# Hyena's filter blocks in single-bank PSUM tiles, its VectorE chain cut finer, and other planner settings, in a one-core hybrid diffusion step

## The chip, the core and the metric

The kernel runs on one core of one Trainium2 chip, as one program. The time is device microseconds (us) of one execution. TensorE (PE in the profile) does the matmuls, VectorE (DVE), ScalarE (ACT) and GpSimd (POOL) the elementwise work, and SyncE (SP) issues the DMAs. Three runs took 1736.06, 1741.65 and 1744.64 us; the median is 1741.65 us.

## The reference

One step of a small backbone with two layers, on 512 latent tokens and 128 context tokens of width 1024 (640 rows, five token tiles of 128). Layer 0 mixes by attention (4 query heads, 2 key/value heads, each 128 wide, with q/k normalisation and rotary) beside a Hyena operator (512 channels); layer 1 is an mLSTM matrix memory with 8 heads, scanned in both directions. Each layer ends with a gated feed-forward block of width 2816. Cut to what the change touches:

```python
proj = x @ w_in                                # q, k, v of the attention and u of Hyena
q = rms_norm(proj[..., :A_Q].reshape(B, L, A_HEADS, A_HEAD_DIM), q_norm)   # k likewise
h = jnp.sin(sin_freq[1] * (h @ w2 + b2))       # Hyena's filters: a small MLP over positions
filt = (h @ w3 + b3).reshape(L, 2, HY_CH) * window[:, None, :]
y = long_conv(v, h_f) + flip(long_conv(flip(v), h_b)) + skip * v    # v = v * x1
out = concatenate([attn, y * x0]) @ w_out
# layer 1, per head and direction, in chunks of 64:
num = w_inter * (C @ q) + (w_intra * (q @ k.T)) @ v
h = num / maximum(abs(den), exp(-mt))
out = (rms_norm(h_f + rev(h_b)) * sigmoid(o)) @ w_out
# both layers: shift, scale and gate rows from silu(c) @ w_mod + b_mod, six sections per layer
```

## The kernel before

All matrix products run in three passes: each fp32 operand is split into a high part (made by ACT, `wh`, `a0h`) and a low part (made by DVE, `wl`, `a0l`), and PE multiplies high by high, high by low and low by high. So PE needs for each 128x1024 block of weights a DMA (`wr`), an ACT cast (`wh`) and a DVE subtraction (`wl`) first.

The stages follow each other on PE: the modulation rows of layer 0 (`mod`), Hyena's twelve projections of 128 channels each (`u4`, `u8`, `u5`, ... for the gate and value, then, after the q/k/v projection `qkv`, `u0` to `u3`), the attention (`s` scores, `pt` transposes of the probabilities, `po` outputs), the output projection, the feed-forward block of layer 0 (`u`, `g`, `dn` there), the mLSTM's projections head by head (`mq`, `mk`, `mo`) with the scans between them, its output projection `o10` onwards, and the feed-forward block of layer 1.

The order of instructions is made when the program is built, by a planner inside the kernel (class `Order`, from L60). It keeps a modelled clock for each engine. The main stream is a list of tasks that issue matmuls (`fm_first`, `fm_task`, `tm_tasks`). Beside it run "sides", generators that issue other work and `yield` between steps: `filter_block` (L1180, Hyena's filters), `forward` (L1112) and the rest of Hyena's long convolution, `qkv_evac` (L1399, the q/k normalisation), the chain of modulation sections (`spawn_mods`, L916), `direction` (L1788, one mLSTM scan) and others. A side's next step is issued once the modelled clocks of DVE and ACT are no further ahead of PE's than the side's lead (`when`, L164). `pump` (L191) starts a further main task early if DVE and ACT are less than a bound ahead; that bound is `TIGHT` while an urgent side is alive. `yield "mm"` and `yield "aux"` wait for a free PSUM tile: there are three two-bank tiles (`mm`) and two single-bank tiles (`aux`), and `od.gave` returns one.

Five places matter for the change. `filter_block` makes `hyf0` to `hyf4`: two matmuls of the filter MLP's last layer, 512 columns each, and two DVE multiplications by the window into `hs` and `hd`. `fm_first` (L523) runs the first three projections (u4, u8, u5) row block by row block, k by k, because its inputs come one k at a time; only the last `TAILK` k are done tile by tile. `forward`, called by `long_conv` with `inverse`, computes the transform of the values; `qkv_evac` evacuates the q/k/v product of a token tile, sums squares on ACT, makes the reciprocal root on DVE (`qn3v` to `qn3y`, eleven small operations) and scales. `direction` makes for head h and direction d the decay weights (`mb`, `w`), the carried state (`dl`, `cb`), the state's part of the output (`it`), the part within the chunk (`in`), the denominator, the sum `hs` and the final state (`pc`); when both directions of a head are done, `head_mix` (L1866) normalises `hs` (`hss`, `hn`), transposes it (`hT`) and multiplies it by the output gate (`mos`).

Of the kernel before, what the change touches and what calls it, by code (L numbers as in the profile page):

```python
# [15 lines left out]
ALU = mybir.AluOpType  # L16
# [43 lines left out]
class Order:  # L60
# [7 lines left out]
    LEAD = 3000.0  # L68
    SPARE = 5000.0
    GUARD = 0.0  # L70
    TIGHT = 2000.0
    FIRST = 2500.0

    def __init__(self):
# [116 lines left out]
    def pump(self):  # L191
        while True:
# [7 lines left out]
            else:  # L200
                spare = self.TIGHT if self.urgent else self.SPARE
                if self.urgent:
# [123 lines left out]
def hybrid_step(ctx: ExitStack, tc: tile.TileContext, A: dict, O: dict):  # L326
    od = Order()
    nc = Bunch(tc.nc, od)
# [16 lines left out]
    def page(name, dt=F32):  # L345
        return pp.tile([P, 648], dt, tag="pg", name=name)
# [7 lines left out]
    def mm(name):  # L354
        t = mmp.tile([P, 1024], F32, tag="mm", name=name)
        od.got("mm", t)
        return t

    def aux(name):
        t = auxp.tile([P, 512], F32, tag="aux", name=name)  # L360
        od.got("aux", t)
        return t

    def MM(out, lhsT, rhs, start=True, stop=True):
        r = nc.tensor.matmul(out, lhsT, rhs, start=start, stop=stop)  # L365
        n = 1
        for d in rhs.shape[1:]:
            n *= d
        k = lhsT.shape[0] / P
        if rhs.dtype == FR:  # L370
            od.issue("PE", max(57.0, 0.4453 * n + 4.0), [out], [lhsT, rhs], 162.0, n / 2.4 * k)
        else:
            od.issue("PE", 2 * max(112.0, n / 1.2 + 4.0), [out], [lhsT, rhs], 165.0, n / 0.6 * k)
# [23 lines left out]
    def rsqrt(ss, n, scale, name, eps=EPS, v=None):  # L397
        y, q, a = (small(name + c, n) for c in "yqa")
        if v is None:
            v = small(name + "v", n)  # L400
            nc.vector.tensor_scalar(v, ss, scale, eps, op0=ALU.mult, op1=ALU.add)
        nc.vector.tensor_scalar(y.bitcast(I32), v.bitcast(I32), -0.5, RSQ, op0=ALU.mult, op1=ALU.add)
        nc.vector.scalar_tensor_tensor(q, v, -0.5, y, op0=ALU.mult, op1=ALU.mult)
        for n in range(3):
            nc.vector.tensor_tensor(a, q, y, op=ALU.mult)
            if n < 2:
                nc.vector.scalar_tensor_tensor(q, a, 1.5, q, op0=ALU.add, op1=ALU.mult)
            nc.vector.scalar_tensor_tensor(y, a, 1.5, y, op0=ALU.add, op1=ALU.mult)
        return y
# [17 lines left out]
                yield  # L427

    EVF = 1
    TAILK = 3  # L430

    def fm_task(src, act, name, evac, needs=()):
        def run(w):
# [89 lines left out]
    def fm_first(specs, act):  # L523
# [9 lines left out]
        def all_(_):  # L533
            ps = []
            for n in range(3):
                od.take("mm")
                ps.append(mm(specs[n][1]))
            seq = [(k, n) for k in range(KT - TAILK) for n in range(3)]
            seq += [(k, n) for n in range(3) for k in range(KT - TAILK, KT)]
            for k, n in seq:  # L540
# [368 lines left out]
    HYE = nc.vector  # L909
    ROPE = nc.gpsimd  # L910
    SLACK1 = 1500.0
    SLACK2 = 2000.0
    SLACK3 = 500.0
    SLACK4 = 500.0

# [110 lines left out]
    def boundary(pss, tiles, l, s, xs, nxt, name, key, pages=None):  # L1026

        n = len(tiles)
        ss = small(name + "ss", n)
        t = {}  # L1030
        yield [("mod", l, s)] + [("mod", 1, 4)] * (l == 0 and s == 5)
        junk = page(name + "j").bitcast(BF)[:, 0:D]
        if WARM and tiles[0] == 0 and nxt is not None:
            nc.scalar.activation(ones1, ones[:, 0:1], AF.Gelu if s == 2 else AF.Exp)
        for j, i in enumerate(tiles):
            if nxt is not None and i >= ROWS:
                t[i] = mw.tile([P, D], F32, tag="mw", name=f"{name}t{i}")
            else:
                t[i] = row(f"{name}t{i}")
            nc.scalar.activation(junk, pss[i], AF.Square, accum_out=ss[:, j : j + 1])  # L1040
            nc.vector.tensor_tensor(t[i], pss[i], mods[l, s, 0 if i < 4 else 1], op=ALU.mult)
            od.gave("mm", pss[i])
            yield 0
        od.side_after(ss)
        yield
        r = rsqrt(ss, n, 1.0 / D, name)
        for j, i in enumerate(tiles):
            nc.vector.scalar_tensor_tensor(xs[i], t[i], r[:, j : j + 1], xs[i], op0=ALU.mult, op1=ALU.add)
            yield 0
            if nxt is None:  # L1050
                nc.sync.dma_start(O["y"][i * P : (i + 1) * P, :], xs[i])
        if nxt is None:
            return
        yield from pre_norm(xs, tiles, l + (s == 5), 3 if s == 2 else 0, nxt, name + "n", key, t, pages)
# [51 lines left out]
    def block(b):  # L1106

        return slice(LS, T) if b == 4 else slice(b, LS, 4)

    hy = {}  # L1110

    def forward(src, cols, out, name):  # L1112
# [24 lines left out]
        for n, (o, x, y, op) in enumerate(((out[0][:, a], c[:, a], c[:, b], ALU.add), (out[0][:, b], c[:, a], c[:, b], ALU.subtract),  # L1137
# [5 lines left out]
            nc.vector.tensor_tensor(o, x, y, op=op)  # L1143
            if FINE and n % FINE == FINE - 1:
                yield 0
        yield

    FINE = 0

    def filters():  # L1150
        z, w = hy["z"], hy["w"]
# [28 lines left out]
    def filter_block(b):  # L1180
        yield ["sin"]
        c = slice(0, HC)
        yield "mm"
        ps = mm(f"hyf{b}")
        for n in range(2):
            MM(ps[:, n * 512 : n * 512 + 512], hy["h"][:, block(b)], hy["w3s"][:, n * 512 : n * 512 + 512])
        load_win(b + 2)
        s_, d_ = page(f"hs{b}"), page(f"hd{b}")
        nc.vector.tensor_tensor(s_[:, c], ps[:, 0:512], hy["win"][b][:, c], op=ALU.mult)
        nc.vector.tensor_tensor(d_[:, c], ps[:, 512:1024], hy["win"][b][:, c], op=ALU.mult)  # L1190
        od.gave("mm", ps)
        hs.append(s_)
        hd.append(d_)

# [2 lines left out]
    def load_win(b):  # L1197
        if b < 5:
            hy["win"][b] = page(f"win{b}")
            nc.sync.dma_start(hy["win"][b][:, 0:HC], A["hy_win"][b])  # L1200
# [111 lines left out]
    def long_conv(hf):  # L1312
# [17 lines left out]
        HYE.tensor_tensor(vp[:, h1], vp[:, h1], gr, op=ALU.mult)  # L1330
        if FINE:
            yield 0
# [8 lines left out]
        for n in range(2):  # L1341
# [4 lines left out]
            HYE.tensor_tensor(S, S, gc, op=ALU.mult)  # L1346
            if FINE:
                yield 0
            nc.vector.tensor_tensor(x[0], x[0], x[1], op=ALU.subtract)
            nc.vector.tensor_tensor(C, C, S, op=ALU.add)  # L1350
            if FINE:
                yield 0
# [41 lines left out]

    QROWS = 2
    QACT = 1
    QSCALE = 1

    def qkv_evac(ps, i):  # L1399
        yield [("qk", j) for j in range(i - QROWS)]  # L1400
# [18 lines left out]
        r = rsqrt(ss, 6, 1.0 / DH, f"qn{i}")  # L1419
        if QSCALE:  # L1420
            for a in range(6):
# [116 lines left out]
    def out_proj(mix, wname, order, l, nxt, xs, halves, name):  # L1538
# [9 lines left out]
        for t in tm_tasks(  # L1548
                lambda k, i, g: [x[:, i * P : (i + 1) * P] for x in cur[k]],
                lambda k: A[wname][order[k] * P : (order[k] + 1) * P, :], KT, halves, name,  # L1550
                lambda ps, t: od.spawn(boundary(ps, t, l, 2, xs, nxt, f"{name}p{t[0]}", "af", name),
                                       lead=BLEAD, urgent=True),
                prep=prep, needs=lambda k, g: [key(q) for q in range(KT)], stay=STAY[l], whole=True,
# [312 lines left out]
    def head_mix(h):  # L1866
# [30 lines left out]
        for d in range(2):  # L1897
            od.spawn(direction(h, d, q, v1, kw[d], ssb, cb[d], hs, co), lead=DLEAD)
        yield [("hs", h)]
# [56 lines left out]
    J1 = 1  # L1956
    QLEAD = 6000.0
    ALEAD = 6000.0
    BLEAD = 4000.0
    FLEAD = 1000.0  # L1960
    MLEAD = 2500.0
    TLEAD = 1500.0
    DLEAD = 1750.0
    OLEAD = 5000.0
    ms = [x for i in range(4) for x in (4 + i, 8 + i)]
    k0, k1 = act_keys("am", 0, HALVES[0]), act_keys("am", 0, HALVES[1])
# [35 lines left out]
    act2 = Lazy("a2")  # L2002
    tasks.append(spawn_mods(SLACK2, (1, 0), (1, 1), (0, 5), (1, 3), (1, 4), keys=[("hid", 0, J0)]))
    tasks += ffn(0, act1, act2, xs)
# [299 lines left out]
```

## Time and profile before

| what | value |
|---|---|
| median of three runs | 1741.65 us |
| the profiled execution | 1739.15 us |
| its span, first to last instruction | 1737.3 us |
| mean granted TensorE clock | 0.987 of full speed |
| PE busy | 1683.4 us, 97% |
| DVE busy | 1243.6 us, 72% |
| ACT busy | 746.3 us, 43% |
| POOL busy | 353.8 us, 20% |

Busy time is the time in which an engine executes; register, branch and semaphore instructions don't count. In the slices of the page each digit is the busy share of one fortieth of the span in tenths. A row of a timeline gives start, duration, engine, line, operation, output and inputs; in square brackets stands how long the engine was idle before it and which engine's result ended that. Nearly all lines are those of helpers (L365 the matmul, L284 everything else), so rows are told apart by the names of their tiles. Granted clock 1.00 is 2.4 GHz and 0.50 is 1.2 GHz.

### The profile page before, as it was taken

To read this page: it belongs to the slowest core of one execution; us is meant where nothing else is said; L and a number is where in the kernel's file an instruction comes from. 1 tells how busy PE (TensorE), PEld (TensorE's weight loads), DVE (VectorE), ACT (ScalarE), POOL (GpSimd) and SP (SyncE) were. 2 spreads that over 40 slices of the span, in tenths; PEclk is the share of its full clock that TensorE was granted. 3 is DMA by queue.
4 is the path that set the end of the run, shared out by engine and by line. 5 is a ranking of instruction groups with operands and counts; after the bars stand their busy time and mean duration, and the time that the engine had idled before them with its cause. 6 is when DMAs were issued, how large, how long until landed. Compare 5 with 4: busy or idle time off the path is not lost. (4 is left out here: it accounts for less than half of the span.)

```text
span 1737.3 us, 25489 instructions
## 1 busy us (share of the span) xinstructions
PE 1683.4 (97%) x10074; PEld 1523.0 (88%) x10074; DVE 1243.6 (72%) x2057; ACT 746.3 (43%) x1233; POOL 353.8 (20%) x187
## 2 busy tenths in 40 slices
PE   7899899999999999999999999997999999999997
PEld 2778787789999999888899999996899999998886
DVE  4788797878878888797766888886578744445365
ACT  3422545545434344455565344334354423333343
POOL 0000121001546454340013111120015411111000
PEclk9999999999999999999999999998999999999999
DMA  9245132412434434454523212122124322223343
GB/s 359 91 152 170 37 101 101 169 38 99 158 121 143 144 119 154 153 198 129 188 89 137 70 47 83 57 69 100 49 77 147 125 77 74 73 74 109 132 159 122
DMA packets 64352, 203.85 MB, mean 117 GB/s; under 512 B 7335, under 2 KB 12455, under 8 KB 64234
## 3 DMA queue, kind: packets, MB, share of 16 engines
q1 hardware_dynamic: 64234, 202.23, 33.9%
q8 instruction: 79, 1.29, 0.3%
q14 instruction: 39, 0.32, 0.1%
HBM read 196.17 MB, written 3.94 MB: 115 GB/s over the span
## 5 line engine op out<-in xcount | busy, mean ns | idle before, releaser
L284 DVE TENSOR_TENSOR wl<-wr,wh 128x1024 fp32r<-128x1024 f32 (+1 forms) x260 | 317.9, 1228 | 107.8 <-ACT wh L284 107.6
L284 ACT CAST wh<-wr 128x1024 fp32r<-128x1024 f32 (+1 forms) x260 | 263.5, 1018 | 146.7 <-PE dn L365 104.1
L284 POOL TENSOR_TENSOR hid<-zg,zu 128x640 f32<-128x640 f32 x44 | 105.5, 2398 | 318.5 <-DVE zu L284 305.9
L284 DVE SCALAR_TENSOR_TENSOR acc<-mw,sc,acc 128x1024 f32<-128x1024 f32 x91 | 168.3, 1868 | 2.7 <-DMA mw<-in_w_mod 2.4
L284 POOL TENSOR_TENSOR acc<-acc,modp 128x1024 f32<-128x1024 f32 x49 | 146.2, 2984 | 115.4 <-ACT modp L284 91.2
L284 DVE SCALAR_TENSOR_TENSOR zg<-g,vec,zg 128x127 f32<-128x127 f32 (+3 forms) x168 | 87.4, 541 | 89.4 <-ACT zg L284 86.4
L365 PE MATMUL dn<-wh,hh 128*128 128x512 f32 x440 | 139.1, 396 | 1.8 <-DVE zu L284 1.6
L365 PE MATMUL dn<-wl,hh 128*128 128x512 f32 x440 | 138.2, 394 | 0.0
L365 PE MATMUL dn<-wh,hl 128*128 128x512 f32 x440 | 138.1, 394 | 0.0
L284 DVE SCALAR_TENSOR_TENSOR zu<-u,vec,zu 128x511 f32<-128x511 f32 (+2 forms) x164 | 86.7, 549 | 62.8 <-ACT zu L284 59.9
L284 ACT ACTIVATE zu<-u,vec 128x640 f32<-128x640 f32 (+1 forms) x42 | 36.8, 876 | 173.8 <-PE u L365 173.8
L365 PE MATMUL u<-a3h,wh 128*128 128x384 f32 (+1 forms) x336 | 104.7, 312 | 0.8 <-DVE a3h L284 0.8
L365 PE MATMUL g<-a3h,wh 128*128 128x384 f32 (+1 forms) x336 | 104.8, 312 | 0.0
L365 PE MATMUL g<-a1h,wh 128*128 128x384 f32 (+1 forms) x336 | 104.8, 312 | 0.0
L365 PE MATMUL u<-a3l,wh 128*128 128x384 f32 (+1 forms) x336 | 104.1, 310 | 0.5 <-POOL a3l L284 0.5
L365 PE MATMUL u<-a3h,wl 128*128 128x384 f32 (+1 forms) x336 | 104.3, 310 | 0.2 <-DVE wl L284 0.2
L365 PE MATMUL u<-a1h,wl 128*128 128x384 f32 (+1 forms) x336 | 104.2, 310 | 0.2 <-DVE wl L284 0.2
L365 PE MATMUL u<-a1h,wh 128*128 128x384 f32 (+1 forms) x336 | 104.2, 310 | 0.0
L365 PE MATMUL g<-a3h,wl 128*128 128x384 f32 (+1 forms) x336 | 104.1, 310 | 0.0
L365 PE MATMUL g<-a3l,wh 128*128 128x384 f32 (+1 forms) x336 | 104.1, 310 | 0.0
L365 PE MATMUL g<-a1h,wl 128*128 128x384 f32 (+1 forms) x336 | 104.0, 310 | 0.0
L365 PE MATMUL u<-a1l,wh 128*128 128x384 f32 (+1 forms) x336 | 104.0, 310 | 0.0
(742 smaller groups left out, 4452.2 us busy)
## 6 DMA issues: line engine op xcount, KB each, us to landing
wr<-in_w_up SPq DMA_DIRECT2D x92, 512.0 KB, 3.3
wr<-in_w_down SPq DMA_DIRECT2D x82, 512.0 KB, 3.3
mw<-in_w_mod SPq DMA_DIRECT2D x80, 512.0 KB, 4.4
wr<-in_w_ml SPq DMA_DIRECT2D x34, 512.0 KB, 3.6
wr<-in_w_out SPq DMA_DIRECT2D x18, 512.0 KB, 4.2
wr<-in_w_in SPq DMA_DIRECT2D x13, 512.0 KB
wr<-in_w_u SPq DMA_DIRECT2D x12, 512.0 KB, 5.2
we<-in_w_mod SPq DMA_DIRECT2D x8, 512.0 KB, 7.3
```

What stands on the lines that cost most here:

```text
L284: r = f(*args, **kw)
L365: r = nc.tensor.matmul(out, lhsT, rhs, start=start, stop=stop)
```

## The change

Seven numbers change, and the body of `filter_block`.

`filter_block` no longer takes one two-bank tile for both halves. It takes a single-bank `aux` tile, issues one 512-column matmul, the multiplication by the window, gives the tile back and yields, and then does the same for the other half. `FINE` 0 to 2 makes `forward` yield after every second of its eight DVE operations, and the rest of the long convolution yield between its parts, so that the planner may put other work in between. `QSCALE` 1 to 0 scales q and k of a token tile by one DVE tensor_tensor of 128x768 instead of six ACT operations of 128x128. `TAILK` 3 to 2: in `fm_first` only the last two k are done tile by tile. `TIGHT` 2000 to 6000, `SLACK2` 2000 to 4000, `BLEAD` 4000 to 6000 and `DLEAD` 1750 to 4000 (all in ns of the modelled clock) let main tasks, the modulation sections (1,0), (1,1), (0,5), (1,3), (1,4), the output projection's boundary and the mLSTM's scans be issued while DVE and ACT are modelled further ahead of PE.

```diff
-    TIGHT = 2000.0
+    TIGHT = 6000.0
...
-    TAILK = 3
+    TAILK = 2
...
-    SLACK2 = 2000.0
+    SLACK2 = 4000.0
...
-    FINE = 0
+    FINE = 2
...
     def filter_block(b):
         yield ["sin"]
         c = slice(0, HC)
-        yield "mm"
-        ps = mm(f"hyf{b}")
-        for n in range(2):
-            MM(ps[:, n * 512 : n * 512 + 512], hy["h"][:, block(b)], hy["w3s"][:, n * 512 : n * 512 + 512])
         load_win(b + 2)
         s_, d_ = page(f"hs{b}"), page(f"hd{b}")
-        nc.vector.tensor_tensor(s_[:, c], ps[:, 0:512], hy["win"][b][:, c], op=ALU.mult)
-        nc.vector.tensor_tensor(d_[:, c], ps[:, 512:1024], hy["win"][b][:, c], op=ALU.mult)
-        od.gave("mm", ps)
+        for n, t in enumerate((s_, d_)):
+            yield "aux"
+            ps = aux(f"hyf{b}{n}")
+            MM(ps, hy["h"][:, block(b)], hy["w3s"][:, n * 512 : n * 512 + 512])
+            nc.vector.tensor_tensor(t[:, c], ps, hy["win"][b][:, c], op=ALU.mult)
+            od.gave("aux", ps)
+            yield 0
...
-    QSCALE = 1
+    QSCALE = 0
...
-    BLEAD = 4000.0
+    BLEAD = 6000.0
...
-    DLEAD = 1750.0
+    DLEAD = 4000.0
```

Since the planner decides the order, the diff alone does not show where instructions go. Three places follow.

**The head, PE.** The first rows of PE before, from the modulation row products (`mod`; `we6`, `we7` are blocks of their weights) to the sums of squares of the inputs (`xss`):

```order
L365 MATMUL mod001_230<-we5_131,sc_93 2x512 x2
L365 MATMUL hyf0_248<-hyw3s_245,hyh1_193 128x512 x2
L365 MATMUL mod001_230<-we6_140,sc_93 2x512 x2
L365 MATMUL mod001_230<-we7_142,sc_93 2x512 x2
L365 MATMUL modt00_275<-vec_84,modr00_121 128x2 x8
```

The same place after the change, and further down, among the first projections (`u8` is tile u8_393; a0h, a0l and wh344, wl345 its operands):

```order
L365 MATMUL mod001_230<-we5_131,sc_93 2x512 x2
L365 MATMUL mod001_230<-we6_140,sc_93 2x512 x2
L365 MATMUL mod001_230<-we7_142,sc_93 2x512 x2
L365 MATMUL modt00_263<-vec_84,modr00_121 128x2 x8
L365 MATMUL xss_284<-ones_88,xq_233 128x1 x5
...
L365 MATMUL u8_393<-a0l0_373,wh1_344 128x384
L365 MATMUL hyf00_412<-hyw3s_245,hyh1_193 128x512
L365 MATMUL hyf01_415<-hyw3s_245,hyh1_193 128x512
```

`hyf0` has left its place between two row products and stands behind the first nine matmuls of the projections; `hyf1` and `hyf2` (not shown) go from behind u4's last matmul into the middle of these projections.

**Hyena's second half, DVE.** Before, from the third part of u0's convolution (`zh0`) to the low part of the weights of u3 (`wl24`); `vx01` to `vm11` are the second half's products with the filter spectrum (`g1c`, `g1s`) and their sums:

```order
L284 SCALAR_TENSOR_TENSOR zh0_1913<-u0_1820,vec_84,zh0_1913 128x127 x2
L284 TENSOR_TENSOR qsq3_1779<-qsq3_1779,qkg_1121 128x768
L284 TENSOR_TENSOR vx01_1873<-vf12_1597,g1c_953 128x512
L284 TENSOR_TENSOR vx11_1874<-vf13_1598,g1s_972 128x512
L284 TENSOR_TENSOR vf12_1597<-vf12_1597,g1s_972 128x512
L284 TENSOR_TENSOR vf13_1598<-vf13_1598,g1c_953 128x512
...
L284 TENSOR_TENSOR vm11_1972<-vf12_1597 128x256
L284 SCALAR_TENSOR_TENSOR zh1_2001<-u1_1919,vec_84,zh1_2001 128x511 x2
L284 SCALAR_TENSOR_TENSOR zh1_2001<-u1_1919,vec_84,zh1_2001 128x127 x2
L284 TENSOR_TENSOR wl24_2015<-wr24_1757,wh24_2014 128x1024
```

The same stretch after the change:

```order
L284 TENSOR_TENSOR qsq4_1802<-qsq4_1802,qn4y_1869 128x768
L284 SCALAR_TENSOR_TENSOR zh0_1903<-u0_1806,vec_84,zh0_1903 128x511 x2
...
L284 TENSOR_TENSOR wl23_1917<-wr23_1720,wh23_1916 128x1024
L284 TENSOR_TENSOR vp01_1947<-vx01_1769 128x256
...
L284 TENSOR_TENSOR qsq3_1791<-qsq3_1791,qkg_1126 128x768
L284 TENSOR_TENSOR qsq4_1802<-qsq4_1802,qkg_1126 128x768
L284 SCALAR_TENSOR_TENSOR zh1_1991<-u1_1909,vec_84,zh1_1991 128x511 x2
L284 SCALAR_TENSOR_TENSOR zh1_1991<-u1_1909,vec_84,zh1_1991 128x127 x2
L284 TENSOR_TENSOR wl24_2005<-wr24_1747,wh24_2004 128x1024
L284 TENSOR_TENSOR vx01_1769<-vf12_1634,g1c_955 128x512
L284 TENSOR_TENSOR vx11_1770<-vf13_1635,g1s_974 128x512
L284 TENSOR_TENSOR vf12_1634<-vf12_1634,g1s_974 128x512
```

`wl24` now stands ahead of the second half's four products with g1, their two sums and the four `vp` and `vm` operations instead of behind these ten; the normalisation of the last token tile (`qsq4`) has come forward, and `wl23`, which stood well ahead of `zh0` before, stands behind it.

**The end of the mLSTM, PE.** Before, from the last matmul of the last gate projection (`mo7`) to the first of the output projection (`o10_0`); `modp` are products for modulation section (1,2):

```order
L365 MATMUL mo7_11153<-a2l7_7690,wh154_10884 128x256
L365 MATMUL in71_11233<-v17_9003,w71_10986 128x129 x4
L365 MATMUL pc71_11254<-kw71_10839,v17_9003 128x128
L365 MATMUL pc71_11254<-v17_9003,kw71_10839 128x1
L365 MATMUL modp1200_11282<-moda120_11262,onesr_91 128x512
L365 MATMUL modp1200_11282<-modb120_11263,onesr_91 128x512
L376 MATMUL hT7_11286<-ident_86,hs7_10917 128x128 x5
L365 MATMUL modp1201_11303<-moda120_11262,onesr_91 128x512
L365 MATMUL modp1201_11303<-modb120_11263,onesr_91 128x512
L365 MATMUL o10_0_11311<-wh155_11016,o1h0_11020 128x512 x2
```

After the change, first where the last head's `in71` has gone (the middle of `mo5`, two gate projections earlier), then the end itself:

```order
L365 MATMUL mo5_10963<-a2l3_7502,wh152_10738 128x256
L365 MATMUL in71_11038<-v17_8988,w71_10933 128x129 x4
L365 MATMUL mo5_10963<-a2h4_7555,wh152_10738 128x256
...
L365 MATMUL mo7_11202<-a2l7_7670,wh154_10957 128x256
L376 MATMUL hT7_11282<-ident_86,hs7_10904 128x128 x5
L365 MATMUL o10_0_11289<-wh155_11081,o1h0_11085 128x512 x2
L365 MATMUL o10_0_11289<-wh155_11081,o1l0_11086 128x512 x2
L365 MATMUL o10_0_11289<-wl155_11082,o1h0_11085 128x512 x2
```

Only the transposes `hT7` are left between `mo7` and `o10`. The scan of head 7 ends some two projections earlier, and section (1,2) of the modulation has moved into the projections `mk5` and `mo2`, four and more projections ahead of `mo5`.

## Rows read from the trace of the kernel before

**Rows 1.** The page: busy time of each engine, share of the span, instructions.

```profile
PE 1683.4 (97%) x10074; PEld 1523.0 (88%) x10074; DVE 1243.6 (72%) x2057; ACT 746.3 (43%) x1233; POOL 353.8 (20%) x187
```

**Rows 2.** What PE waited for: us in total, times, longest.

```profile
PE modp L365 <- ACT moda L284: 6.3, 1, 6.3
PE qkv L365 <- DVE wl L284: 4.4, 1, 4.4
PE u L365 <- DVE wl L284: 3.5, 3, 3.1
```

**Rows 3.** Timeline of PE at hyf0 and hyf1.

```profile
24.80 3.43 PE L365 MATMUL hyf<-hyw3s,hyh 128*128 128x512 f32 x4 [2.85 <-DVE hyw3s L284]
...
78.37 2.08 PE L365 MATMUL hyf<-hyw3s,hyh 128*128 128x512 f32 x4 [2.29 <-DVE zh L284]
```

**Rows 4.** Windows of PE: stretch, length, PE busy (instructions), granted clock, DMA share, GB/s.

```profile
74.00:84.00 10.00, 7.71 (x43) 1.00 0.36 131
180.00:190.00 10.00, 5.56 (x22) 0.83 0.36 105
250.00:260.00 10.00, 6.85 (x34) 0.83 0.15 52
```

**Rows 5.** Timeline of ACT, then DVE, behind u4's last matmul.

```profile
73.83 1.05 ACT L284 CAST wh<-wr 128x1024 fp32r<-128x1024 f32 x1 [3.20 <-PE u L365]
...
76.05 2.17 DVE L284 SCALAR_TENSOR_TENSOR zh<-u,vec,zh 128x511 f32<-128x511 f32 x4
```

**Rows 6.** Timeline of DVE ahead of wl24.

```profile
242.03 0.95 DVE L284 TENSOR_TENSOR qsq<-qsq,qkg 128x768 f32<-128x768 f32 x1
242.90 2.06 DVE L284 TENSOR_TENSOR vx<-vf,g1c 128x512 f32<-128x512 f32 x1
...
247.72 0.68 DVE L284 TENSOR_TENSOR vf<-vf,g1c 128x512 f32<-128x512 f32 x1
...
252.95 1.22 DVE L284 TENSOR_TENSOR wl<-wr,wh 128x1024 fp32r<-128x1024 f32 x1
```

**Rows 7.** Timeline of DVE and ACT where the attention starts.

```profile
260.29 1.29 DVE L284 TENSOR_TENSOR vx<-vp,vp 128x512 f32<-128x512 f32 x2
...
260.41 1.86 ACT L284 ACTIVATE qsq<-qsq,qn4y 128x128 f32<-128x128 f32 x6 [8.53 <-DVE qn4y L284]
...
266.76 2.18 DVE L284 SCALAR_TENSOR_TENSOR zh<-u,vec,zh 128x511 f32<-128x511 f32 x4 [1.52 <-ACT zh L284]
...
269.11 0.82 DVE L284 TENSOR_REDUCE mx<-s 128x1 f32<-128x640 f32 x1
```

**Rows 8.** Windows, all engines: PE, PEld, DVE, ACT, POOL busy, granted clock, DMA share, GB/s.

```profile
190.00:262.00 72.00, 68.64 (x383) 61.35 (x381) 61.92 (x139) 38.77 (x121) 15.03 (x10) 0.98 0.21 68
932.00:1168.00 236.00, 235.45 (x1728) 233.82 (x1727) 195.40 (x467) 98.45 (x195) 49.17 (x32) 1.00 0.22 72
```

**Rows 9.** Timeline of PE at the end of the mLSTM.

```profile
1182.36 1.06 PE L365 MATMUL in<-v,w 128*128 128x129 f32 x8
...
1194.06 1.30 PE L376 MATMUL hT<-ident,hs 128*128 128x128 f32 x5 [2.00 <-DVE hs L284]
...
1196.01 1.05 PE L365 MATMUL o<-wh,o1h 128*128 128x512 f32 x2
...
1200.42 0.39 PE L365 MATMUL modp<-moda,onesr 128*128 128x512 f32 x1
...
1200.88 0.62 PE L365 MATMUL o<-wh,o1h 128*128 128x512 f32 x2
...
1202.27 0.40 PE L365 MATMUL modp<-moda,onesr 128*128 128x512 f32 x1
```

**Rows 10.** Timeline of ACT, POOL and DVE behind mo7, the last gate.

```profile
1183.40 0.69 ACT L284 ACTIVATE mos<-mo 128x640 f32<-128x640 f32 x1
...
1184.17 1.49 POOL L284 TENSOR_SCALAR mos<-mos 128x640 f32<-128x640 f32 x1 [7.70 <-ACT mos L284]
...
1195.47 0.88 DVE L284 SCALAR_TENSOR_TENSOR mos<-hT,vec,mos 128x640 f32<-128x640 f32 x1 [0.96 <-PE hT L376]
```

## The prediction before the run

> **What bounds the kernel now.** I read the page first. PE is busy for 97% of the span, DVE for 72%, ACT for 43% [rows 1]. So the matmuls themselves set the end, and the change touches none of their number; only the 3% in which PE stands, and the time in which it runs at half clock, can be won. I then listed what PE waits for, longest first. Three places make most of it: the modulation product at the end of the mLSTM, a `qkv` matmul that lacks its `wl`, and a Hyena projection that lacks its `wl` [rows 2]; to them come the two waits of the filter blocks [rows 3]. Last I read windows for the clock: after the long waits the granted clock of ten microseconds is 0.83, that is about 3.4 us at 1.2 GHz and the rest at 2.4 GHz [rows 4]. A matmul stream that runs through those 3.4 us loses half of them, 1.7 us. After the shorter wait of 2.29 us the window shows 1.00. So a wait of 3 us costs nearly 5, and one of 2.3 costs itself.
>
> **The change part by part.** The sum is made against the profiled execution, 1739.15 us, which lies 2.5 us under the median of the runs, 1741.65.
>
> *Filter blocks, TAILK, the head.* `hyf0` makes PE stand for 2.85 us and then runs for 3.43 us where the equal `hyf1` takes 2.08, so 1.35 us go to the half clock; `hyf1` stands for 2.29 us because all three two-bank tiles are taken and u4's has to be evacuated first [rows 3]. In the new order `hyf0` comes after the first projections' matmuls, when its operand is long there, and `hyf1` and `hyf2` use single-bank tiles, so the three items go: 2.85 + 1.35 + 2.29 = 6.5 us. Against it stands TAILK. From u4's last matmul (the ACT cast that it releases, 73.83) to the end of its DVE evacuation (76.05 + 2.17 = 78.22) pass 4.4 us [rows 5]. Then the next projection can have u4's tile. With two k per tile left, the two other tiles cover it with four k. A matmul of such a stream takes 0.136 us on the mean (235.45 us for 1728, rows of the mLSTM, [rows 8]), a projection of 48 so 6.5 us and one of its eight k 0.82: the cover is 3.3 us, and 1.1 are missing. DVE is nearly full there, and I take another 0.9 us for a `wl` that comes late behind the moved multiplications. Head: 6.5 - 2.0 = 4.5 us gained; the ends are 2 and 6.5.
>
> *FINE, the wait for wl24.* Before, DVE does ten operations of the second half between `zh0` and `zh1`; one of them takes 2.06 us where a like one takes 0.68, and `wl24` starts only at 252.95 [rows 6]. PE stands 3.1 us for it [rows 2], so from about 251 us on, and then runs 3.4 us at half clock [rows 4]: 4.8 us in all. In the new order the ten stand behind `wl24`. Between `zh0` and `wl24` remain `wl23`, four `vp` and `vm`, two multiplications of 0.95 us and `zh1`; but the last token tile's root and its scaling have come forward ahead of `zh0`. Added up from the rows, `wl24` ends around 250.7 in the old time, 0.4 us before PE wants it. Any one operation on the way that is stretched like the 2.06 row takes that slack. I take 4.0 us gained; the ends are 0 and 4.8. The wait for `wl` at 181 us [rows 2] keeps its DVE order and stays, with its half clock.
>
> *QSCALE.* Six ACT operations, 1.86 us a tile [rows 7], become one DVE operation of the shape of the 0.95 us row [rows 6], five times: 4.75 us more on DVE, 9.3 us less on ACT. From 190 to 262 us DVE is busy for 61.9 of 72 us [rows 8], so it has room for this on the average, and I put it at nothing; the cover is PE's own stream, and if DVE comes late at a `wl`, each late microsecond is PE's.
>
> The Trainium skill (Perfetto Trace Analysis, Optimizing Scalar/DVE Operations) says that work which either engine can do may go to ScalarE when VectorE is the saturated one. That speaks against this edit; the 86% of the row is near it, not at it. What it would make here is the second rival.
>
> *The start of the attention.* Before, four sums of Hyena (`vx`, and a like pair for `vz`, 1.29 us a pair, from 260.29 on) are done ahead of `zh3`, and the first score maximum follows `zh3` at 269.11 [rows 7]. In the new DVE order these four stand between `zh3` and the maximum: 2.5 us later after u3's end. PE's filler there, Hyena's inverse product, needs the same sums. So the first probabilities reach PE about 2.5 us later, and with what PE waits here already the wait is near 3 us, long enough for the half clock, 1.7 us more: 4.2. Later waits in this stage may shorten, as inverse products become filler there, so I take a loss of 4.0 us; ends: a loss of 6 and a gain of 2.
>
> *DLEAD and SLACK2, the end of the mLSTM.* This is the largest term. `mo7` ends at 1182.36 and the first `o10` matmul starts at 1196.01: 13.65 us [rows 9]. In between PE stands for 6.3 us for section (1,2)'s `moda` [rows 2], which waits on ACT behind the squares of head 7, and 2.0 us for the normalised `hs`. Then the first six `o10` steps take 4.41 us (1196.01 to 1200.42), where three take 1.39 at full clock (1200.88 to 1202.27), six 2.79: 1.62 us to the half clock. Two `modp` products, 0.46 us each, stand between `o10` steps. In the new order only `hT7` is left, 5 transposes, 0.65 us at full clock. Gained: 13.65 - 0.65 + 1.62 + 0.92 = 15.54 us. What is moved must still be done: `in71` and `pc71` 1.4 us, four `modp` products 1.85 us. That leaves 12.3 us. A new wait comes: the third tile of `o10` needs the PSUM tile that `hT7` holds until the gate is multiplied in. That is `mo7`'s tanh, POOL's 1.49 us and 0.88 us on DVE [rows 10], with their starts about 4.2 us after `mo7`, and the tile is wanted at 0.65 + 2.79 = 3.4 us; with a `wl` of 1.22 us that may stand ahead on DVE I take 1.2 us. Gain 11.1 us; ends 7 and 12.3. The condition is that head 7's scan, now issued two and a half projections, 16 us, before `mo7` ends, finishes in time: before, from `in71` to `hT7` it took 12 us (1182.36 to 1194.06), so it has 4 us to spare.
>
> *DLEAD in heads 0 to 6.* PE is busy for 235.45 of 236 us here, at full clock, DVE for 195.4 [rows 8]. There is nothing to win. A scan that is issued with DVE further behind holds its PSUM tile longer. I take nothing; ends: no gain, and a loss of 1 us a head, 8 in all.
>
> *BLEAD, TIGHT elsewhere.* The order of PE through the first feed-forward block is almost the same; I take nothing, plus or minus 2.
>
> Sum: 4.5 + 4.0 - 4.0 + 11.1 = 15.6 us, so 1723.5 for the profiled execution and 1726.0 by the median. I state 1725.
>
> **The rivals.** First, the tail pays half: the scan of head 7 or the weights' `wl` of `o10` come late because DVE is full, and the new wait is 6 us instead of 1.2. For it: DVE is the busiest helper, and heads are ended closer together. Against: 4 us to spare. 1725 + 5 = 1730.
>
> Second, the DVE load decides between 190 and 330 us: QSCALE's 4.75 us come out at the `wl`s, so the 4.0 of the third projection are lost and the attention starts 4.75 us later. 1725 + 4 + 4.75 = 1733.8. For it: 86% busy, and only 0.4 us of slack at `wl24`. Against: ACT is relieved, so the chain to the scaled q is 0.9 us shorter a tile. By the rule of the Trainium skill named above this is the case to expect where DVE is full.
>
> Third, gains are given back in the heads: 1 us a head and two half-clock stretches, 8 + 3.4 = 11.4 us. 1736.5, not to be told from no change (for this kernel about 0.5%, 1733 to 1750, is no change).
>
> Fourth, slower: a scan's tiles (`it`, `in`) are taken while DVE is modelled 4 us behind, and with three two-bank tiles the next projection finds none. If that makes PE stand for 2.85 us once a head, the smallest wait here that a half clock followed, it costs 4.55 x 8 = 36 us: 1725 + 36 = 1761. It decides from 25 / 8 = 3.1 us a head on. Against it: a projection takes 6.5 us, and a tile would have to be held for that long. For it: in this stage no wait for a tile is seen before, so the trace gives no measure.
>
> The Trainium skill (TensorE: Matmul & The Clock Gate, A second HAM failure mode: psum-queue depth-cycling) says that a PE which idles for moments between groups while it cycles through PSUM banks can drop its clock again and again. The stage's row with clock 1.00 at 99.8% busy shows none of that before; it would make the fourth case dearer.
>
> Fifth, better: the attention loses nothing and PE finds all `wl`s in time, 4 to 9 us more: 1718.
>
> **How the numbers follow.** Forecast 0.50 (its own range 1718 to 1731), tail half 0.13, DVE load 0.13, given back in the heads 0.12, better 0.06, slower 0.06. Faster by over 0.5% means below 1733: the forecast, the better case, most of the tail case (0.10) and half of the DVE case (0.07), 0.73. Slower 0.06. No change 0.21. The range for 8 in 10 takes in the first four cases and part of the better one, with a few microseconds for the unknown ends: 1712 to 1740.
>
> **What would show it.** In the new profile: the longest waits of PE are the first DMA and the `qkv` wait at some 177 us; no wait for `hyw3s` and none of 2 us for a tile at `hyf`. u3's wait for `wl` is under 1.5 us. A wait of 2 to 4 us stands ahead of the first `pt`, with a half-clock stretch behind it. `mo7` to `o10` is under 1 us, with about 1 us before the third tile, and the clock there is 1.00. Windows of the heads stay above 99% busy. I would be wrong if `it`, `in` or `o10` show new waits of some microseconds, or if `wl23` or `wl24` are still waited for as long as now.

## The result, and the profile after

The changed kernel takes 1730.23 us (median of five runs, 1725.98 to 1734.29), the kernel before 1740.36 (five runs beside it). The ratio is 0.9942, with a 95% interval of 0.9917 to 0.9967: 10 us faster. The forecast was 1725 with a range of 1712 to 1740. The profiled execution of the changed kernel took 1730.52 us, its span is 1728.7.

The first view is the list of what PE waited for in the changed kernel (us in total, times, longest); the first wait of all, 6.7 us for a DMA, and some smaller ones are left out.

```profile
...
PE dn L365 <- DVE zu L284: 3.5, 2, 2.9
PE xss L365 <- DVE xq L284: 3.1, 1, 3.1
PE qkt L376 <- DVE qsq L284: 2.9, 1, 2.9
...
PE qkv L365 <- DVE wl L284: 1.8, 1, 1.8
...
PE u L365 <- DVE wl L284: 1.4, 2, 1.2
PE modp L365 <- ACT moda L284: 1.4, 1, 1.4
...
PE u L365 <- DVE zh L284: 1.1, 1, 1.1
PE modp L365 <- DVE modb L284: 0.9, 1, 0.9
...
PE o L365 <- DVE mos L284: 0.8, 1, 0.8
```

Beside [rows 2]: the wait of 6.3 us for `moda` is gone, that for `wl` at u3 too (the 1.2 us left are u2's). New are three waits of about 3 us, for `zu`, `xq` and `qsq`. To see what each stage won or lost I cut both spans at the same landmarks of PE's stream. The windows of the changed kernel (stretch, length, PE busy, granted clock) are, from the head to the end: up to the first `qkv`; to u3's end; the attention; its output projection and the boundary; the second product of the first feed-forward block; the heads of the mLSTM; its end with the output projection; the rest. (Two stretches are left out: the first product of the first feed-forward block and the start of the mLSTM.)

```profile
0.00:145.60 145.60, 131.73 (x605) 0.96 0.55 197
145.60:258.00 112.40, 109.41 (x575) 0.95 0.33 113
258.00:323.20 65.20, 56.85 (x372) 0.97 0.17 63
323.20:396.50 73.30, 70.36 (x321) 0.98 0.31 101
705.30:871.60 166.30, 162.83 (x719) 0.98 0.50 165
930.70:1191.70 261.00, 260.38 (x1909) 1.00 0.24 77
1191.70:1251.30 59.60, 58.83 (x266) 1.00 0.27 93
1251.30:1728.70 477.40, 467.94 (x2802) 1.00 0.31 105
```

The same of the kernel before, for the third projection, the attention, the second product of the first feed-forward block and the end of the mLSTM:

```profile
147.90:265.70 117.80, 109.76 (x590) 0.97 0.28 92
265.70:324.30 58.60, 52.92 (x359) 1.00 0.28 100
701.70:862.80 161.10, 159.88 (x719) 1.00 0.53 173
1182.50:1256.70 74.20, 65.48 (x286) 0.91 0.20 69
```

Length less busy time is the idle time of a stage; of the last stage the 8.8 us behind the last matmul, which both kernels have, are not counted. From the clock in windows of 2 us I worked out what the half clock cost beside it, to about 0.2 us: half of the busy time that ran at 1.2 GHz. Worked out so for both kernels (us):

```
stage                        idle + half clock, before    after     gain   forecast
head, to the first qkv              15.2 + 6.9          13.9 + 4.8   3.4      4.5
qkv and u0 to u3                     8.0 + 3.3           3.0 + 5.1   3.2      4.0
attention                            5.7 + 0.0           8.4 + 1.7  -4.4     -4.0
output projection, boundary          0.7 + 0.0           2.9 + 1.5  -3.7      0
feed-forward 0, second product       1.2 + 0.0           3.5 + 3.0  -5.3      0
start of the mLSTM (mv)              1.8 + 1.9           1.9 + 0.0   1.8      0
heads                                0.6 + 1.5           0.6 + 0.0   1.5      0
end of the mLSTM, o10               8.7 + 3.5           0.8 + 0.0  11.4     11.1
feed-forward 1                       3.0 + 0.0           0.7 + 0.0   2.3      0
sum (with the rest)                 45.1 + 17.1         35.7 + 16.1 10.4     15.6
```

Two of the gains, 1.8 us at the start of the mLSTM and 1.5 in its heads, are chance: they are one stretch at half clock in the profile before (6.8 us long, from 919.7 on), and the run b_dlead below, in which the rows come in the same order up to there, has none.

The end of the mLSTM is the gain. On PE, from `hT7` to the third `o10` tile, in answer to [rows 9]:

```profile
1191.55 0.71 PE L376 MATMUL hT<-ident,hs 128*128 128x128 f32 x5
1192.01 0.71 PE L365 MATMUL o<-wh,o1h 128*128 128x512 f32 x2
...
1194.47 0.63 PE L365 MATMUL o<-wl,o1h 128*128 128x512 f32 x2
1195.87 0.73 PE L365 MATMUL o<-wh,o1h 128*128 128x512 f32 x2 [0.77 <-DVE mos L284]
```

and on DVE the gate's multiplication that frees the tile, in answer to [rows 10]:

```profile
1193.48 0.82 DVE L284 TENSOR_TENSOR o1l<-mos,o1h 128x640 fp32r<-128x640 f32 x1
1194.93 0.88 DVE L284 SCALAR_TENSOR_TENSOR mos<-hT,vec,mos 128x640 f32<-128x640 f32 x1 [0.63 <-POOL mos L284]
```

13.65 us from `mo7` to `o10` have become the half microsecond of `hT7`; the wait for the third tile is there, 0.77 us; the clock is full. The stretch from 1185 to 1200 us, before and after:

```profile
1185.00:1200.00 15.00, 7.53 (x20) 0.54 0.33 111
```

```profile
1185.00:1200.00 15.00, 14.23 (x82) 1.00 0.50 175
```

### The profile page after: what moved, and what is told of

It reads as the page before. It is cut to its first block, busy times and chain, and to the rows that moved or that the text cites. A ratio compares the mean times of both kernels' runs of the same rounds, so it can differ in the third digit from the quotient of the medians.

```text
span 1728.7 us, 25447 instructions
## 1 busy us (share of the span) xinstructions
PE 1684.2 (97%) x10074; PEld 1523.0 (88%) x10074; DVE 1246.8 (72%) x2062; ACT 737.6 (43%) x1203; POOL 352.6 (20%) x187
## 5 line engine op out<-in xcount | busy, mean ns | idle before, releaser
L284 DVE TENSOR_TENSOR wl<-wr,wh 128x1024 fp32r<-128x1024 f32 (+1 forms) x260 | 325.2, 1257 | 108.9 <-ACT wh L284 108.6
L365 PE MATMUL g<-a1l,wh 128*128 128x384 f32 (+1 forms) x336 | 104.2, 310 | 0.0
```

Of the source, the lines that this page charges most:

```text
L284: r = f(*args, **kw)
```

## The experiments

All runs were compared with the kernel before on the same chip; ratios are to it (its medians beside them lie between 1739.1 and 1740.8).

| run | edit | median us | ratio, 95% interval |
|---|---|---|---|
| after_again | the changed kernel | 1730.81 | 0.9957 (0.9942 to 0.9972) |
| b_dlead | before, DLEAD 4000 | 1727.70 | 0.9939 (0.9918 to 0.9959) |
| a_dlead | after, DLEAD 1750 | 1738.98 | 1.0000 (0.9985 to 1.0016) |
| a_slack2 | after, SLACK2 2000 | 1727.52 | 0.9928 (0.9902 to 0.9955) |
| a_qscale | after, QSCALE 1 | 1740.45 | 1.0007 (0.9993 to 1.0020) |
| a_fine | after, FINE 0 | 1730.17 | 0.9951 (0.9937 to 0.9965) |
| a_tight | after, TIGHT 2000 | 1737.26 | 0.9981 (0.9964 to 0.9998) |
| a_tight_again | the same | 1736.36 | 0.9966 (0.9948 to 0.9984) |
| a_fb | after, old filter blocks | 1728.92 | 0.9943 (0.9925 to 0.9962) |
| b_fb | before, new filter blocks | 1744.51 | 1.0024 (1.0010 to 1.0039) |
| c_fbsl | after, old filter blocks, SLACK2 2000 | 1724.20 | 0.9904 (0.9884 to 0.9925) |
| c_q7 | after, SLACK2 2000, QLEAD 7000 | 1726.91 | 0.9921 (0.9899 to 0.9943) |

**The end of the mLSTM: DLEAD alone.**

```diff
-    DLEAD = 1750.0
+    DLEAD = 4000.0
```

> The kernel before with DLEAD 4000 and nothing else. Theory A (the end of the mLSTM pays for the change, and DLEAD alone moves it): PE goes from mo7 to o10 within 1 us instead of 13.5, the third o10 tile waits about 0.8 us, the heads stay over 99% busy, and the time falls by 11 us, 1740.4 to 1729. Rival B (scans issued earlier cost the heads what the end saves, and the change's gain is the head's and Hyena's): the heads show new waits of 0.5 us or more each, and the time is 1736 to 1740.

> The changed kernel with DLEAD back at 1750. Theory A: the waits for moda, modb and hs at the end of the mLSTM come back, 8 us idle and the half clock, and the whole gain goes: 1730.2 + 11 = 1741. Rival B: 1731 to 1734, since the gain lies elsewhere.

Theory A holds on both sides: with this one number the old kernel falls to 1727.7, 11.4 less than beside it, and without it the changed kernel is as slow as before (8.2 us above after_again, where 11 were expected). In the waits of the changed kernel with DLEAD 1750 the old ones stand again beside the new ones:

```profile
PE modp L365 <- ACT moda L284: 6.6, 2, 6.3
PE dn L365 <- DVE zu L284: 3.5, 2, 2.9
PE hT L376 <- DVE hs L284: 2.0, 1, 2.0
```

In the run b_dlead PE idles 0.6 us in the heads as before, 0.6 in the whole end. So the scans issued earlier cost nothing where they went. And all the other edits together bring nothing: a_dlead is they alone.

**Are the waits those of one execution?**

> The changed kernel once more, as it is. Theory A: its profile again has waits near 2.9 us for zu in the first feed-forward block, 2.3 us for the modulation product ahead of it, 2.9 us for qsq where the attention starts, 3.1 us for xq in the head; the time is 1730 as before. Rival B: these waits differ by 1.5 us or more between executions, so that one profile can't place the losses.

Theory A: in the second profile the waits for `zu`, `xq` and `qsq` are 2.91, 3.08 and 2.93 us, the same to 0.01 us. The `modp` wait differs by a third of a microsecond (it hangs on a DMA), and the `qkv` wait moved between 1.8 and 3.2. That wait and the clock make up for each other: it ends at 183.8 us in the first execution and at 183.9 in the second, and ahead of it the half clock, from 168 us on, lasted 6.8 us in the first and 3.4 in the second, so that PE came later and waited less. What differs most between executions is the clock, of which below.

**SLACK2 and the wait for zu.**

```diff
-    SLACK2 = 4000.0
+    SLACK2 = 2000.0
```

> The changed kernel with SLACK2 back at 2000. In the first feed-forward block the changed kernel loses about 5 us (a wait of 2.9 us of dn for zu on DVE, and the half clock behind it). Theory A (SLACK2 lets modulation sums stand ahead of zu on DVE, so zu is late): the wait falls under 1.2 us, no half clock there, and the time falls by 4 to 5 us to about 1726. Rival B (the wait is that of one execution, from how DVE and POOL happen to meet): dn waits for about as long, or the wait is gone in the unchanged rerun too; the time stays within 1.5 us of 1730.

In the changed kernel a modulation sum (2.47 us) stands on DVE between `zg` and `wl`, and `hl` behind it is stretched to 2.76 us:

```profile
701.48 2.47 DVE L284 SCALAR_TENSOR_TENSOR acc<-mw,sc,acc 128x1024 f32<-128x1024 f32 x1
703.88 1.21 DVE L284 TENSOR_TENSOR wl<-wr,wh 128x1024 fp32r<-128x1024 f32 x1
705.02 2.76 DVE L284 TENSOR_TENSOR hl<-hid,hh 128x384 fp32r<-128x384 f32 x1
707.70 1.27 DVE L284 SCALAR_TENSOR_TENSOR acc<-mw,sc,acc 128x1024 f32<-128x1024 f32 x1
708.90 2.17 DVE L284 SCALAR_TENSOR_TENSOR zu<-u,vec,zu 128x511 f32<-128x511 f32 x4
```

With SLACK2 at 2000 the first sum is gone from there, `hl` takes 0.54 us, and PE waits 0.91 us instead of 2.91:

```profile
703.54 2.44 DVE L284 TENSOR_TENSOR wl<-wr,wh 128x1024 fp32r<-128x1024 f32 x1
705.91 0.54 DVE L284 TENSOR_TENSOR hl<-hid,hh 128x384 fp32r<-128x384 f32 x1
...
707.57 2.16 DVE L284 SCALAR_TENSOR_TENSOR zu<-u,vec,zu 128x511 f32<-128x511 f32 x4
...
709.88 0.70 PE L365 MATMUL dn<-wh,hh 128*128 128x512 f32 x2 [0.91 <-DVE zu L284]
```

So the wait is SLACK2's (theory A). In time it brought 2.7 to 3.3 us by the medians, where 4 to 5 were expected, and the two intervals overlap. The profiled execution took the longest of its six (1734.68 us); it has half clock in that stage too, but from 801 us on, far behind `zu`. Two more versions with SLACK2 at 2000, c_fbsl and c_q7 below, idle 1.8 and 1.7 us in this stage with the clock full, where the eight profiles with 4000 idle 3.5 to 4.0. During the long `hl` POOL worked too, an addition that took 3.23 us (704.14 to 707.37), where the like one before took 2.40. The Trainium skill (SBUF — State Buffer, Who interferes with whom) says that a VectorE instruction with two SBUF inputs and a GpSimd one that reads SBUF exclude each other at a shared port. The rows agree: `hl` takes 2.76 us beside POOL's addition and 0.54 without it, and in a_slack2, where the addition ran from 702.52 to 704.91, `wl` beside it took 2.44 instead of 1.21. No run took POOL's addition away, so that this is the cause stays argued.

**QSCALE.**

```diff
-    QSCALE = 0
+    QSCALE = 1
```

> The changed kernel with QSCALE back at 1 (q and k scaled by six ACT operations). In the changed kernel PE waits 2.9 us for the rotated qsq where the attention starts and then runs at half clock; the stage from u3's end to the last attention output idles 8.4 us against 5.7 before. Theory A (the five added DVE operations make that chain late): the wait for qsq falls under 1 us, the stage's idle time to about 5.7, the time by 3 to 4 us to 1727. Rival B (FINE's order of the Hyena sums makes it late): the wait stays near 2.9 us and the time near 1730.5.

Both theories fall. Putting the scaling back on ACT costs 10 us. The attention then idles 13.2 us instead of 8.4, with these waits among others:

```profile
263.11 1.22 PE L365 MATMUL iy<-dfi,vx 128*128 128x128 f32 x4 [4.35 <-DVE vx L284]
...
268.81 0.90 PE L376 MATMUL qkt<-ident,qsq 128*128 128x128 f32 x3 [1.56 <-DVE qsq L284]
```

The number also moves the order of the Hyena sums, of the normalisation and of everything behind them, so the 10 us come with another order; what the six ACT operations cost by themselves no run shows. The kernel before had QSCALE 1 and an attention that idled 5.7 us.

**FINE.**

```diff
-    FINE = 2
+    FINE = 0
```

> The changed kernel with FINE back at 0. Theory A (FINE took the 3.1 us wait for wl24 away, and its half clock): the wait of u3 for wl comes back, 3 us, and the stage from the first qkv product to u3's end loses 3 to 5 us; where the order of the sums is also to blame for the attention's start, that wins back up to 4 there: 1730 to 1735. Rival B (the wait went because QSCALE moved the normalisation): no wait for wl24 over 1.5 us, 1727 to 1731.

Rival B: the time stays, 1730.2. The wait for `wl24` does not come back, so it is not FINE's yields alone that took it away (nor is it shown that QSCALE did); instead the wait for `qsq` at the attention's start is longer, 4.2 us:

```profile
PE qkt L376 <- DVE qsq L284: 4.2, 1, 4.2
```

**TIGHT.**

```diff
-    TIGHT = 6000.0
+    TIGHT = 2000.0
```

> The changed kernel with TIGHT back at 2000: the order of PE differs only in the transposes of the boundary behind the first feed-forward block. Theory A (TIGHT is neutral, as predicted): within 1.5 us of 1730.5, idle time of the first feed-forward block's second product 3.5 us as in the changed kernel. Rival B (TIGHT brings a part of the 5 us lost there): the idle time there falls to under 2 us and the time to 1726 to 1728.

> The changed kernel with TIGHT back at 2000, once more, on another occasion: the first time its twelve runs lay between 1728 and 1741, median 1737, and the profiled one was among the fastest and shows no new wait. Theory A (the slow runs belong to this order): the median is again 1735 or more. Rival B (chance of that occasion): 1731 within 2 us, as TIGHT changes nothing that the trace shows.

Neither theory of the first run holds, and the second run confirms the first (theory A): medians of 1737.3 and 1736.4, with twelve runs each from 1727 to 1741 in two clumps, near 1728 and near 1738. The two profiles are of one clump each (spans 1727.0 and 1736.9) and have one order of instructions. Idle time differs by 2 us, the half clock by 8.5. The windows of the shorter one, then of the longer one, around the first boundary and the start of the mLSTM:

```profile
345.00:360.00 15.00, 13.13 (x55) 1.00 0.04 17
915.00:945.00 30.00, 29.17 (x193) 0.94 0.38 123
```

```profile
345.00:360.00 15.00, 12.35 (x40) 0.77 0.09 35
915.00:945.00 30.00, 29.19 (x183) 0.83 0.38 124
```

So TIGHT 6000 is worth about 6 us by the medians and 4 by the means of all runs, which I did not forecast; the intervals of the ratios overlap. PE's order differs behind the first feed-forward block and, unlike what was expected, also at the start of feed-forward 1. There both profiles with TIGHT 2000 wait 1.4 us in all (0.47 and 0.31 for `a3l`, 0.66 for `o1p3ny`), and the two of the changed kernel don't. The rest is the clock. Why it is lower more often with TIGHT 2000 isn't settled: the windows show where, not what decides it.

**The filter blocks.** Back to the two-bank tile in the changed kernel, and the new form alone in the old one:

```diff
-        for n, t in enumerate((s_, d_)):
-            yield "aux"
-            ps = aux(f"hyf{b}{n}")
+        yield "mm"
+        ps = mm(f"hyf{b}")
+        for n in range(2):
...
```

> The changed kernel with the old filter blocks, one two-bank tile each. Theory A (the single-bank tiles gain in the head): idle time and half-clock loss up to the first qkv product go from 18.7 back to about 22 us, a wait of 2.3 us of a filter block for a tile comes back, and the time rises by 3 us to 1733.5. Rival B (the head gains nothing by them, since the wait for xq took the place of the wait for hyw3s and TAILK made a new wait for u4's tile): within 1 us of 1730.5 or lower.

> The kernel before with the new filter blocks and nothing else. Theory A (the single-bank tiles pay in the head): the waits for hyw3s, 2.85 us, and for u4's tile, 2.29 us, are gone, idle time and half-clock loss up to the first qkv product fall from 22 to 18 us, and the time from 1739.5 to 1735 or 1736. Rival B (other waits take their place, the wait for xq above all, and the rest of Hyena is disturbed): within 1.5 us of 1739.5, or above.

Rival B, twice: without them the changed kernel takes 1728.9, no slower; alone they make the old kernel slower by 0.24%. In the head the waits for `hyw3s` and for u4's tile do go, but PE reaches `xss` earlier and finds DVE's squares missing. In the changed kernel:

```profile
31.62 1.65 PE L365 MATMUL xss<-ones,xq 128*128 128x1 f32 x7 [3.08 <-DVE xq L284]
...
54.64 0.45 PE L365 MATMUL u<-a0h,wh 128*128 128x384 f32 x1 [1.66 <-ACT a0h L284]
```

2.85 us for `hyw3s` are replaced by 3.08 for `xq` (0.43 before); the first `u` comes only 1.3 us earlier. Idle time and half clock of the head are 20.3 us in b_fb and 19.2 in a_fb, against 22.1 before and 18.7 after. Alone, the blocks also bring the attention and the boundary from 6.4 to 13.9 us of loss. This holds in all profiles: the four with two-bank blocks (before, b_dlead, a_fb, c_fbsl) idle 5.0 to 5.7 us in the attention and 0.7 to 2.1 at the boundary, at full clock; the ten with single-bank blocks idle 6.3 to 13.2 and 1.8 to 4.0, all of them with half clock in the attention.

**Two combinations.** Both are the changed kernel with SLACK2 back at 2000, the first also with the old filter blocks (the edit above), the second with

```diff
-    QLEAD = 6000.0
+    QLEAD = 7000.0
```

> The changed kernel with the old filter blocks and SLACK2 back at 2000, to see whether what the attention and the first feed-forward block lost can be had back together. Theory A (the two add up): attention idle near 5 us as with the old filter blocks, the dn wait for zu under 1.2 us as with the old SLACK2, 1725 to 1726. Rival B (the wait for wl24 that is back with the old filter blocks, 3.6 us, eats it): 1728 to 1730.

> The changed kernel with SLACK2 back at 2000 and the lead of the q/k normalisation (QLEAD) 7000 instead of 6000: wl24 still stands ahead of the products with g1, and the rotated qsq of token tile 3 comes five rows ahead of zh3 instead of one. Theory A (the wait of 2.9 us for qsq at the attention's start is a matter of this row order): it falls under 1.5 us, the attention idles under 7 us, and with the dn wait under 1.2 us the time is 1722 to 1725, better than all others. Rival B (the sums vx and vz behind zh3 still make the first scores late, so that another wait takes its place): attention idle 8 us as before, 1727 to 1729.

c_fbsl has the lowest median of all, 1724.2 us in four runs (0.9904; theory A): the attention idles 5.0 us, `zu` is waited for 0.97, and the wait of 3.6 us for `wl24` is back. It beats the kernel before; against the rerun of the changed one (0.9957) the intervals don't overlap, against its first runs (0.9942) and against b_dlead they do. c_q7 does half of what theory A wanted: the wait for `qsq` falls to 1.58 us and the attention's idle time to 6.3, but u3 waits 1.7 us for `wl24` and the boundary 3.4 us for `modp`; 1726.9 is no better than SLACK2 alone.

## Why the prediction was right, and where it was not

The sign, the range and the main term were right. The four largest terms of the sum:

*The end of the mLSTM.* 11.1 us forecast, 11.4 measured in the stage, 11.4 by DLEAD alone. The new wait at the third `o10` tile was 0.8 us, by the working 4.2 less 3.4; I had raised it to 1.2. The term was headed DLEAD and SLACK2; it is DLEAD alone, which moves `modp` and the scan of head 7 both.

*The head.* 4.5 forecast, 3.4 measured. Of its steps, the two waits of the filter blocks went, and TAILK's new wait came where it was put, at 1.07 us against the 1.1 worked out. The step that failed is that the wait for `hyw3s` leaves nothing behind: `xss` is late next, as the rows above show. I did not ask when DVE would be done with the squares. And 3.4 us of the 6.9 that the half clock cost before lay at 124 to 131 us, in a stretch without any wait, behind 32 products of one column each. After the change that stretch is gone, and one as long stands behind 32 like products in the next stage (last section): so much of the head's gain moved on and was not won. A wait's price was off too: that one of 2.3 us costs itself was read from one profile, and in b_dlead the same wait of 2.29 us has 3.4 us at half clock, from 78.3 us on.

*The wait for wl24.* 4.0 forecast, 3.2 for the stage. This agreement is in part luck: the wait and its half clock went, 3.15 and 1.7 us, and the wait of `qkv`, which I had left as it was, fell from 4.4 to 1.8; against them stand the 3.4 us of half clock just named and u2's wait. The wait for `wl24` went as worked out, and the slack of 0.4 us was real: `wl24` ended at 250.5, stretched to 2.48 us, and u2's `wl23`, moved behind `zh0`, cost 1.2 us. That the step is FINE's was wrong: with FINE at 0 the wait stays away, with the old filter blocks it is back at 3.6 us, and the new blocks alone keep it at 3.2 (b_fb). No single edit was shown to move `wl24` ahead of the products.

*The attention's start.* A loss of 4.0 forecast, 4.4 measured, with the half clock. The place was wrong. PE does not wait ahead of the first `pt`; it waits for the rotated `qsq` of token tile 3, 2.93 us right behind u3, since u3 now ends earlier and DVE is busy without a break:

```profile
257.74 0.28 PE L365 MATMUL u<-a0l,wh 128*128 128x256 f32 x1
260.95 0.85 PE L376 MATMUL qkt<-ident,qsq 128*128 128x128 f32 x6 [2.93 <-DVE qsq L284]
```

```profile
250.44 2.05 DVE L284 TENSOR_TENSOR vx<-vf,g1c 128x512 f32<-128x512 f32 x1
...
259.78 0.55 DVE L284 TENSOR_TENSOR qsq<-qsq,qrt 128x384 f32<-128x384 f32 x1
260.25 0.55 DVE L284 TENSOR_TENSOR qsq<-qsq,qru 128x384 f32<-128x384 f32 x1
260.72 2.17 DVE L284 SCALAR_TENSOR_TENSOR zh<-u,vec,zh 128x511 f32<-128x511 f32 x4
```

So the gain of the third projection is what is lost here: the same queue is late a few rows on. The runs trade one wait for the other (`wl24` and `qsq`): 3.6 us and 0.4 in a_fb, 1.7 and 1.6 in c_q7, none and 2.9 in the changed kernel. The edit behind the loss is the filter blocks, which the prediction did not connect with this stage: with the old ones the changed kernel's attention idles 5.1 us at full clock.

*What was put at nothing.* Here the 5 us between forecast and result lie. SLACK2 (no term of its own outside the end) cost the wait for `zu`; the boundary lost 3.7 us by waits of `modp`, which wander with the landing of a DMA but come with the new filter blocks (with the old ones the changed kernel idles 1.4 us there, and the new ones alone bring the old kernel from 0.7 to 5.2 with the half clock). Feed-forward 1 gained 2.3, of it 1.4 with TIGHT; the 3.3 us at the start of the mLSTM and in its heads were chance. QSCALE at nothing and TIGHT at nothing were both wrong in the changed kernel's surroundings: taking either back costs 10 us and 4 to 6. BLEAD was right: with 4000 the program has its rows in the same order on PE, DVE and ACT.

The rivals: the second, that the added DVE work decides, was named for QSCALE with the Trainium skill's rule behind it (Perfetto Trace Analysis, Optimizing Scalar/DVE Operations). Its place, DVE between 190 and 330 us, is where the gain of the third projection went. Nothing shows QSCALE as its cause: the version with the scaling on ACT is 10 us slower here, and a_fb, with the scaling on DVE, idles less in the attention than the kernel before; the measurement decides. The first and the third did not happen: the wait for the third `o10` tile was 0.8 us, and the heads idle 0.6 us at full clock. Nor did the fourth, that scans hold the PSUM tiles: those 0.6 us are the same in both kernels. Of the signs, `qkv` as the longest wait beside the first DMA failed: `zu`, `xq` and `qsq` are longer.

## What to carry to other kernels

Before a wait is booked as gained, look for what the waiting engine needs next and when that is ready; `hyw3s` handed its wait to `xq`, `wl24` handed its to `qsq`. A single number in a planner is tested alone and taken away alone: here one of seven numbers carried all of the gain, and a version without two of the other edits has the lowest median. At the end of a stage, where the main stream waited for a chain of small operations of a last head, an earlier issue was nearly free here.

## What the runs showed of the hardware

The clock falls also where no wait is long. In the longer execution with TIGHT 2000 it is low after waits of 0.88 and 0.73 us at the start of the mLSTM, for about 10 us; in the changed kernel the same two waits (0.88 and 0.76) have no half clock behind them:

```profile
915.00:930.00 15.00, 14.15 (x113) 1.00 0.42 148
```

In the changed kernel's profile it is low at 165 to 175 us while PE is busy throughout, but with products of one column before it falls at 167.6 (`modt`, of a modulation section):

```profile
165.00:175.00 10.00, 10.00 (x45) 0.66 0.19 54
```

```profile
164.48 3.98 PE L365 MATMUL modt<-ones,acc 128*128 128x1 f32 x32
```

Every profile has two such rows of 32, near 120 and near 165 us, without a wait at either. Behind the first the clock falls in before, b_dlead, b_fb, a_fb and c_fbsl, and in none of the nine others; behind the second in all but before and a_fb. So a busy PE does not by itself keep the clock; why it falls behind one row of them and not behind the other, no run shows.

Between the two profiles with TIGHT 2000, which have one order of instructions, the half clock makes 8.5 us of the 9.9 by which their spans differ. What sets it off in one execution and not in the other, no run here shows.
